# Row sums of a 16384 x 1024 matrix: two load queues, and VectorE adding each row as two halves

## The chip, the cores and the metric

The kernel runs on one core of a Trainium2 chip. The metric is device time in microseconds (us) of one execution; lower is better. Times of several executions are given by their median.

## The reference

```
x: 32 x 512 x 1024 float32, divisor: 1024.0
out = sum(x over the last axis) / divisor        # 32 x 512 float32
```

There are 32 x 512 = 16384 rows of 1024 numbers, 67.1 MB to be read, and 16384 numbers to be written.

## The kernel before

The rows are spread over the 128 partitions, 128 rows to each. "A row" below means one row in every partition: 128 x 1024 float32, 0.524 MB. The 128 rows are split into three parts by their place in DRAM: `x_main` (97 rows, results in `res`), `x_first` (15 rows, results in `res0`) and `x_last` (16 rows, results in `fin`). Within a part, a partition's rows of one load are one contiguous run in DRAM.

The loads are listed in `loads`, in the order of work. The main part is loaded in pieces of 2, 13, five times 14, and 12 rows, the first part in one piece of 15, and the last part in pieces of 9, 4 and 2 rows. Pieces of the main and the first part, and the 9 rows, go round three buffers, `bulk[0]` to `bulk[2]`; the 4 and the 2 rows have buffers of their own, `t4` and `t2`. The very last row comes as two halves, `pa` and `pb`.

All loads are issued by SyncE (SP), on its one queue. The first three are moved by `start_loads_at_once` ahead of everything else in the program (L119 in the profile). Each later load into a `bulk` buffer (L146) waits until VectorE, and ScalarE where it had rows of it, have finished the load that was in that buffer three loads ago. The loads of `t4`, `t2`, `pa` and `pb` (L146 to L148) wait for nothing, but are issued after the 9 rows.

VectorE handles the loads in their order, after a wait for each to land. A piece of the main or the first part is summed by one reduction over all its rows:

```
nc.vector.reduce_sum(out=dst[:, :m], in_=t[:, :m, :], axis=AX).then_inc(dve)      # L191
```

The rows of the last part are summed one by one by `both_halves` (L182): one instruction reads the two halves of a row as two inputs, adds them element by element, scales, writes the sums over the first half, and accumulates them to one number.

ScalarE takes the last few rows of some loads (the second number in the pairs of `main`, `first` and `last`: 3 of the 12, 6 of the 15, 4, 2 and 1 of the last part): an activation with a copy and an accumulated sum into `junk` (L174), one row each.

The sums of the main and the first part are not yet scaled. GpSimd multiplies `res` by 1/divisor (L159) when its rows are done, and `res0` (L163) after that; SyncE waits for each and then issues its store (L150, L152). The last store, of `fin` (L207), waits for VectorE and ScalarE.

Of the kernel before, what the change touches and what calls it, by code (L numbers as in the profile page):

```python
# [7 lines left out]
F32 = mybir.dt.float32  # L8
ADD = mybir.AluOpType.add
COPY = mybir.ActivationFunctionType.Copy  # L10
AX = mybir.AxisListType.X
SP = mybir.EngineType.SP


# [20 lines left out]
@with_exitstack  # L35
def kernel(
    ctx: ExitStack,
    tc: tile.TileContext,
    x: bass.AP,
    divisor: float,  # L40
    out: bass.AP,
):
    nc = tc.nc
    nc.at_finalize(start_loads_at_once)
    xf = x.flatten_outer_dims()
    N, D = xf.shape
    P = nc.NUM_PARTITIONS
    scale = 1.0 / float(divisor)
    J = N // P
    assert J * P == N  # L50

    F, L = 15, 16
    M = J - F - L
    W = M + L
    x_first = bass.AP(tensor=x.tensor, offset=0, ap=[[F * D, P], [D, F], [1, D]])
    x_main = bass.AP(tensor=x.tensor, offset=P * F * D, ap=[[W * D, P], [D, M], [1, D]])
    x_last = bass.AP(tensor=x.tensor, offset=P * F * D + M * D, ap=[[W * D, P], [D, L], [1, D]])
    o_first = bass.AP(tensor=out.tensor, offset=0, ap=[[F, P], [1, F]])
    o_main = bass.AP(tensor=out.tensor, offset=P * F, ap=[[W, P], [1, M]])
    o_last = bass.AP(tensor=out.tensor, offset=P * F + M, ap=[[W, P], [1, L]])  # L60

    def room(name, *shape):
        return nc.alloc_sbuf_tensor(name, [P, *shape], F32).ap()


    base = -(-nc.sbuf_base // 32) * 32
    room("pad", -base % 1024 // 4)
    assert nc.sbuf_base % 1024 == 0
    c = 512
    bulk = [room(f"bulk{i}", r, D) for i, r in enumerate((14, 14, 15))]  # L70
    t4 = room("t4", 4, D)
    t2 = room("t2", 2, D)
    pa = room("pa", c)
    pb = room("pb", D - c + 16)[:, : D - c + 2]
    res0 = room("res0", F)
    res = room("res", M)
    fin = room("fin", L)
    junk = [nc.alloc_psum_tensor(f"junk{i}", [P, D], F32).ap() for i in range(4)]

    loads = []
    sems = {}

    def sem(name):
        sems[name] = nc.alloc_semaphore(name)
        return sems[name]

    in_bulk = [sem(f"in_bulk{i}") for i in range(3)]
    in_t4, in_t2, in_pa, in_pb = (sem(f"in_{n}") for n in ("t4", "t2", "pa", "pb"))  # L90
    out_first, out_main = sem("out_first"), sem("out_main")
    dve, act, pool = sem("by_dve"), sem("by_act"), sem("by_pool")
    landed = nc.alloc_semaphore("landed")

    n = 0
    main = [(2, 0), (13, 0)] + [(14, 0)] * 5 + [(12, 3)]
    first = [(15, 6)]
    last = [(9, 4), (4, 2), (2, 1)]
    assert sum(r for r, _ in first) == F
    assert sum(r for r, _ in main) == M and sum(r for r, _ in last) == L - 1  # L100
    for part, src, dst, by in (
        (main, x_main, res, 1.0), (first, x_first, res0, 1.0), (last, x_last, fin, scale)
    ):
        j = 0
        for rows, on_act in part:
            if rows > 4:
                t, s, slot = bulk[n % 3][:, :rows, :], in_bulk[n % 3], n
                n += 1
            elif part is main:
                t, s, slot = bulk[n % 3][:, :rows, :], in_bulk[n % 3], n  # L110
                n += 1
            else:
                t, s, slot = (t4, in_t4, None) if rows == 4 else (t2, in_t2, None)
            loads.append((t, s, src[:, j : j + rows, :], on_act, dst[:, j : j + rows], by, slot))
            j += rows


    for t, s, src, *_ in loads[:3]:
        i = nc.sync.dma_start(out=t, in_=src).then_inc(s, 16)  # L119
        tc.no_tile_sem_insts.add(i.ins.name)  # L120
    tc.close()
    tc.compile()  # L122


    done_dve, done_act = {}, {}
    d = a = 0
    for k, (t, s, src, on_act, dst, by, slot) in enumerate(loads):
        rows = t.shape[1]
        d += 1 if by == 1.0 else rows - on_act
        a += on_act  # L130
        done_dve[k], done_act[k] = d, a
    arrived, seen = [], {}
    for t, s, *_ in loads:
        seen[s.num] = seen.get(s.num, 0) + 16
        arrived.append(seen[s.num])


    for k, (t, s, src, on_act, dst, by, slot) in enumerate(loads):
        if k < 3:
            continue  # L140
        if slot is not None:
            nc.sync.wait_ge(dve, done_dve[k - 3])
            if done_act[k - 3]:
                nc.sync.wait_ge(act, done_act[k - 3])
            nc.sync.wait_ge(s, arrived[k] - 16)
        nc.sync.dma_start(out=t, in_=src).then_inc(s, 16)  # L146
    nc.sync.dma_start(out=pa, in_=x_last[:, L - 1, :c]).then_inc(in_pa, 16)  # L147
    nc.sync.dma_start(out=pb[:, : D - c], in_=x_last[:, L - 1, c:]).then_inc(in_pb, 16)  # L148
    nc.sync.wait_ge(pool, 2)
    nc.sync.dma_start(out=o_main, in_=res).then_inc(out_main, 16)  # L150
    nc.sync.wait_ge(pool, 3)
    nc.sync.dma_start(out=o_first, in_=res0).then_inc(out_first, 16)  # L152


    nc.gpsimd.memset(pb[:, D - c :], 0.0).then_inc(pool)  # L155
    k = len(main) - 1
    nc.gpsimd.wait_ge(dve, done_dve[k])
    nc.gpsimd.wait_ge(act, done_act[k])
    nc.gpsimd.tensor_scalar_mul(out=res, in0=res, scalar1=scale).then_inc(pool)  # L159
    k += len(first)  # L160
    nc.gpsimd.wait_ge(act, done_act[k])
    nc.gpsimd.wait_ge(dve, done_dve[k])
    nc.gpsimd.tensor_scalar_mul(out=res0, in0=res0, scalar1=scale).then_inc(pool)  # L163


    a = 0
    for k, (t, s, src, on_act, dst, by, slot) in enumerate(loads):
        rows = t.shape[1]
        for r in range(rows - on_act, rows):
            if r == rows - on_act:  # L170
                nc.scalar.wait_ge(s, arrived[k])
            if a >= len(junk):
                nc.scalar.wait_ge(act, a - len(junk) + 1)
            nc.scalar.activation(  # L174
                junk[a % len(junk)], t[:, r, :], COPY, scale=by, accum_out=dst[:, r : r + 1]
            ).then_inc(act)
            a += 1


    def both_halves(dst, src, by):  # L180
        h = src.shape[-1] // 2
        return nc.vector.tensor_tensor_reduce(  # L182
            out=src[:, :h], in0=src[:, :h], in1=src[:, h:], scale=by, scalar=0.0,
            op0=ADD, op1=ADD, accum_out=dst,
        )

    for k, (t, s, src, on_act, dst, by, slot) in enumerate(loads):
        m = t.shape[1] - on_act
        nc.vector.wait_ge(s, arrived[k])
        if by == 1.0:  # L190
            nc.vector.reduce_sum(out=dst[:, :m], in_=t[:, :m, :], axis=AX).then_inc(dve)  # L191
        else:
            for r in range(m):
                both_halves(dst[:, r : r + 1], t[:, r, :], by).then_inc(dve)
    nc.vector.wait_ge(in_pa, 16)
    nc.vector.wait_ge(pool, 1)
    both_halves(pb[:, D - c : D - c + 1], pa, 1.0).then_inc(dve)
    d += 1
    nc.vector.wait_ge(in_pb, 16)
    nc.vector.wait_ge(dve, d)  # L200
    both_halves(fin[:, L - 1 :], pb, scale).then_inc(dve)
    d += 1


    nc.sync.wait_ge(dve, d)
    nc.sync.wait_ge(act, a)
    nc.sync.dma_start(out=o_last, in_=fin).then_inc(landed, 16)  # L207
    for s in (out_first, out_main):
        nc.sync.wait_ge(s, 16)
    ids = [s.num for s in sems.values()]  # L210
    assert max(ids) - min(ids) + 1 == len(ids)
    nc.sync.sem_clear(range(min(ids), max(ids) + 1))
    nc.sync.wait_ge(landed, 16).then_inc(landed, -16)
# [35 lines left out]
```

## Time and profile before

| what | us |
|---|---|
| three runs, median (lowest to highest) | 160.63 (160.36 to 160.64) |
| the profiled execution | 160.41 |
| its span, from first to last instruction | 159.1 |
| VectorE (DVE) busy, 29 instructions | 117.1 |
| ScalarE (ACT) busy, 33 instructions | 18.5 |
| GpSimd (POOL) busy, 7 instructions | 1.0 |
| one reduction of 14 rows on VectorE | 15.1 |
| one row on ScalarE, activation alone | 1.01 |

The profile page counts the time in which an engine works as busy; waits, branches and the issuing of DMAs are not counted. Lines of groups name the source line, the engine, the operation, what is written and read, with partitions x elements, and in square brackets the idle time just before and what ended it. "SPq" is SyncE's own instruction queue, which issues the DMAs. The chain of waits follows the work back from the last instruction, at each step to what released it.

### The profile page before, as it was taken

To read this page: it belongs to the slowest core of one execution; us is meant where nothing else is said; L and a number is where in the kernel's file an instruction comes from. 1 tells how busy PE (TensorE), PEld (TensorE's weight loads), DVE (VectorE), ACT (ScalarE), POOL (GpSimd) and SP (SyncE) were. 2 spreads that over 40 slices of the span, in tenths; PEclk is the share of its full clock that TensorE was granted. 3 is DMA by queue.
4 is the path that set the end of the run, shared out by engine and by line. 5 is a ranking of instruction groups with operands and counts; after the bars stand their busy time and mean duration, and the time that the engine had idled before them with its cause. 6 is when DMAs were issued, how large, how long until landed. Compare 5 with 4: busy or idle time off the path is not lost.

```text
span 159.1 us, 141 instructions
## 1 busy us (share of the span) xinstructions
DVE 117.1 (74%) x29; ACT 18.5 (12%) x33; POOL 1.0 (1%) x7
## 2 busy tenths in 40 slices
DVE  0500089966999599959996899959999960399743
ACT  3000000000000000000000000000008000392684
POOL 0000000000000000000000000000000010000000
DMA  7999969999999699999997899999995999699894
GB/s 286 459 482 455 453 303 461 461 461 461 461 461 433 288 433 461 461 461 461 461 447 332 375 461 461 461 396 395 482 556 247 494 494 494 297 445 445 371 410 159
DMA packets 2448, 67.18 MB, mean 422 GB/s; under 512 B 656, under 2 KB 656, under 8 KB 912
## 3 DMA queue, kind: packets, MB, share of 16 engines
q1 hardware_dynamic: 2448, 67.18, 98.2%
HBM read 67.11 MB, written 0.07 MB: 422 GB/s over the span
## 4 chain that ended last, share of the span: by engine, by line
DMA 77%; DVE 21%; SPq 1%; issue 0%
DMA bulk<-in_x_dram 55%; DMA pb<-in_x_dram 22%; DVE res L191 20%; SPq L146 1%; SPq L147 0%; DVE pb L182 0%; DVE fin L182 0%
## 5 line engine op out<-in xcount | busy, mean ns | idle before, releaser
L191 DVE TENSOR_REDUCE res<-bulk 128x14 f32<-128x14336 f32 (+3 forms) x9 | 111.2, 12360 | 36.3 <-DMA bulk<-in_x_dram 36.3
L174 ACT ACTIVATE junk<-bulk 128x1024 f32<-128x1024 f32 x13 | 13.1, 1010 | 135.3 <-DMA bulk<-in_x_dram 135.3
L182 DVE CUSTOM_DVE_ANT_0 t<-t 128x512 f32<-128x512 f32 x3 | 2.0, 689 | 2.9 <-DMA t<-in_x_dram 2.9
L182 DVE CUSTOM_DVE_ANT_0 bulk<-bulk 128x512 f32<-128x512 f32 x5 | 3.1, 689 | 1.1 <-DMA bulk<-in_x_dram 1.1
L174 ACT ACTIVATE junk<-t 128x1024 f32<-128x1024 f32 x3 | 3.1, 1021 | 0.9 <-DMA t<-in_x_dram 0.9
L174 ACT ACTIVATION_READ_ACCUMULATOR junk<-bulk 128x1 f32 x13 | 2.4, 186 | 0.0
L174 ACT ACT_TABLE_LOAD x1 | 1.3, 1283 | 2.4 <-PEq L122 2.4
L159 POOL TENSOR_SCALAR res<-res 128x97 f32<-128x97 f32 x1 | 0.5, 465 | 127.4 <-DVE res L191 127.4
L182 DVE DVE_READ_ACCUMULATOR2_ANT fin<- 128x1 f32 x9 | 0.7, 82 | 0.0
L174 ACT ACTIVATION_READ_ACCUMULATOR junk<-t 128x1 f32 x3 | 0.6, 187 | 0.0
L182 DVE CUSTOM_DVE_ANT_0 pb<-pb 128x257 f32<-128x257 f32 x1 | 0.4, 427 | 0.2 <-DMA pb<-in_x_dram 0.2
L182 DVE CUSTOM_DVE_ANT_0 pa<-pa 128x256 f32<-128x256 f32 x1 | 0.4, 425 | 0.0
L163 POOL TENSOR_SCALAR res<-res 128x15 f32<-128x15 f32 x1 | 0.3, 262 | 17.3 <-DVE res L191 17.3
L155 POOL MEMSET pb<- 128x2 f32 x1 | 0.1, 99 | 2.0 <-POOLq L122 2.0
L230 POOL MEMSET const-bfloat16-1.0<- 128x1 bf16 x1 | 0.1, 101 | 0.0
L230 POOL MEMSET const-uint8-127<- 128x1 uint8 x1 | 0.1, 101 | 0.0
L230 POOL MEMSET const-float32-0.0<- 128x1 f32 x1 | 0.1, 99 | 0.2 <-issue 0.2
L230 POOL MEMSET const-float32-1.0<- 128x1 f32 x1 | 0.1, 98 | 0.0
L182 DVE DVE_READ_ACCUMULATOR2_ANT pb<- 128x1 f32 x1 | 0.1, 80 | 0.0
## 6 DMA issues: line engine op xcount, KB each, us to landing
bulk<-in_x_dram SPq DMA_DIRECT2D x5, 7168.0 KB, 36.4
bulk<-in_x_dram SPq DMA_DIRECT2D x1, 7680.0 KB, 34.5
bulk<-in_x_dram SPq DMA_DIRECT2D x1, 6656.0 KB, 19.9
bulk<-in_x_dram SPq DMA_DIRECT2D x1, 6144.0 KB, 33.2
bulk<-in_x_dram SPq DMA_DIRECT2D x1, 4608.0 KB, 28.4
t<-in_x_dram SPq DMA_DIRECT2D x1, 2048.0 KB, 32.9
bulk<-in_x_dram SPq DMA_DIRECT2D x1, 1024.0 KB, 4.7
t<-in_x_dram SPq DMA_DIRECT2D x1, 1024.0 KB, 34.9
```

Of the source, the lines that this page charges most:

```text
L146: nc.sync.dma_start(out=t, in_=src).then_inc(s, 16)
L155: nc.gpsimd.memset(pb[:, D - c :], 0.0).then_inc(pool)
L159: nc.gpsimd.tensor_scalar_mul(out=res, in0=res, scalar1=scale).then_inc(pool)
L163: nc.gpsimd.tensor_scalar_mul(out=res0, in0=res0, scalar1=scale).then_inc(pool)
L174: nc.scalar.activation(junk[a % len(junk)], t[:, r, :], COPY, scale=by, accum_out=dst[:, r : r + 1]).then_inc(act)
L182: return nc.vector.tensor_tensor_reduce(out=src[:, :h], in0=src[:, :h], in1=src[:, h:], scale=by, scalar=0.0, op0=ADD, op1=ADD, accum_out=dst,
L191: nc.vector.reduce_sum(out=dst[:, :m], in_=t[:, :m, :], axis=AX).then_inc(dve)
L230: nc = _bacc.Bacc("TRN2", target_bir_lowering=False, num_devices=1)
```

## The change

Loads are now issued by two engines. The list `order` names for each load its queue, SyncE (`sp`) or ScalarE (`sc`), its part, its rows and how many of them are ScalarE's. The first load is 7 rows from SyncE; then 14-row loads alternate between ScalarE and SyncE; the 15 rows of `x_first` are the last load of ScalarE's queue, and 6 rows of the main part follow on SyncE's. The loads of the last part are as before, on SyncE's queue. The three buffers go round as before, so a load waits for VectorE to finish the load three places ahead of it in `order`, on the engine that issues it. Of the first three loads the two on SyncE are moved ahead of the program; ScalarE's first one is not.

VectorE sums every row with `both_halves`, already scaled. ScalarE keeps only the rows of the last part. GpSimd's two multiplications go, and the stores of `res` and `res0` wait for VectorE instead.

```diff
-    bulk = [room(f"bulk{i}", r, D) for i, r in enumerate((14, 14, 15))]
+    bulk = [room(f"bulk{i}", r, D) for i, r in enumerate((14, 15, 14))]
...
-    main = [(2, 0), (13, 0)] + [(14, 0)] * 5 + [(12, 3)]
-    first = [(15, 6)]
-    last = [(9, 4), (4, 2), (2, 1)]
...
+    sp, sc = nc.sync, nc.scalar
+    order = [(sp, x_main, res, 7, 0)]
+    order += [(sc, x_main, res, 14, 0), (sp, x_main, res, 14, 0)] * 3
+    order += [(sc, x_first, res0, 15, 0), (sp, x_main, res, 6, 0)]
+    order += [(sp, x_last, fin, 9, 4), (sp, x_last, fin, 4, 2), (sp, x_last, fin, 2, 1)]
...
-    for t, s, src, *_ in loads[:3]:
+    early = [k for k, load in enumerate(loads[:3]) if load[0] is sp]
+    for k in early:
+        _, t, s, src, *_ = loads[k]
         i = nc.sync.dma_start(out=t, in_=src).then_inc(s, 16)
...
-        if slot is not None:
-            nc.sync.wait_ge(dve, done_dve[k - 3])
-            if done_act[k - 3]:
-                nc.sync.wait_ge(act, done_act[k - 3])
-            nc.sync.wait_ge(s, arrived[k] - 16)
-        nc.sync.dma_start(out=t, in_=src).then_inc(s, 16)
+        if slot is not None and k > 2:
+            queue.wait_ge(dve, done_dve[k - 3])
+            queue.wait_ge(s, arrived[k] - 16)
+        queue.dma_start(out=t, in_=src).then_inc(s, 16)
     nc.sync.dma_start(out=pa, in_=x_last[:, L - 1, :c]).then_inc(in_pa, 16)
     nc.sync.dma_start(out=pb[:, : D - c], in_=x_last[:, L - 1, c:]).then_inc(in_pb, 16)
-    nc.sync.wait_ge(pool, 2)
+    nc.sync.wait_ge(dve, max(done_dve[k] for k, load in enumerate(order) if load[2] is res))
     nc.sync.dma_start(out=o_main, in_=res).then_inc(out_main, 16)
-    nc.sync.wait_ge(pool, 3)
     nc.sync.dma_start(out=o_first, in_=res0).then_inc(out_first, 16)
...
-    nc.gpsimd.tensor_scalar_mul(out=res, in0=res, scalar1=scale).then_inc(pool)
...
-    nc.gpsimd.tensor_scalar_mul(out=res0, in0=res0, scalar1=scale).then_inc(pool)
...
         nc.vector.wait_ge(s, arrived[k])
-        if by == 1.0:
-            nc.vector.reduce_sum(out=dst[:, :m], in_=t[:, :m, :], axis=AX).then_inc(dve)
-        else:
-            for r in range(m):
-                both_halves(dst[:, r : r + 1], t[:, r, :], by).then_inc(dve)
+        for r in range(t.shape[1] - on_act):
+            both_halves(dst[:, r : r + 1], t[:, r, :], scale).then_inc(dve)
```

## The prediction

> **What bounds the kernel now.** I read the chain of waits first, then the order of time on VectorE, then the DMA parts of the page, each to answer one question: what ends last, is the thing that ends last ever idle, and what would have to be late for the end to move.
>
> The chain, its last pieces (start, length, what):
>
> ```profile
> 105.00 15.10 DVE res L191
> ...
> 121.97 35.17 DMA pb<-in_x_dram
> 157.15 0.02 issue
> 157.17 0.43 DVE pb L182
> 157.60 0.01 DVE fin L182
> ```
>
> The last half row lands at 157.15 and VectorE needs 0.43 us more. The 20% of VectorE in this chain is not a price: the chain passes through a reduction because a load was issued when it ended, but that load then lay in the queue for 35 us. Whether it delayed any data is seen in the landings. In the timeline, VectorE's start after a wait on a DMA is a landing:
>
> ```profile
> 4.72 2.29 DVE L191 TENSOR_REDUCE res<-bulk 128x2 f32<-128x2048 f32 x1 [4.72 <-DMA bulk<-in_x_dram]
> ...
> 37.30 15.09 DVE L191 TENSOR_REDUCE res<-bulk 128x14 f32<-128x14336 f32 x1 [2.89 <-DMA bulk<-in_x_dram]
> ...
> 105.00 24.75 DVE L191 TENSOR_REDUCE res<-bulk 128x14 f32<-128x14336 f32 x2 [1.83 <-DMA bulk<-in_x_dram]
> ...
> 148.58 0.69 DVE L182 CUSTOM_DVE_ANT_0 bulk<-bulk 128x512 f32<-128x512 f32 x1 [1.10 <-DMA bulk<-in_x_dram]
> 149.20 0.08 DVE L182 DVE_READ_ACCUMULATOR2_ANT fin<- 128x1 f32 x1
> 149.20 0.69 DVE L182 CUSTOM_DVE_ANT_0 bulk<-bulk 128x512 f32<-128x512 f32 x1
> ```
>
> From 37.30 to 105.00 four loads of 14 rows land: 67.70 / 56 = 1.209 us a row (a row here is one row in each of 128 partitions, 0.524 MB, so 434 GB/s). All 128 rows at that pace take 154.7 us. The first load of 2 rows landed at 4.72 where 2.42 us of streaming would do, so starting cost 2.30 us. 2.30 + 154.7 = 157.0, and the last data came at 157.15. Nothing was lost between: loads stream without a gap that can be measured, and VectorE waits for every load (1.8 us before each of the 14-row ones). The page says the same in its own way:
>
> ```profile
> DVE 117.1 (74%) x29; ACT 18.5 (12%) x33; POOL 1.0 (1%) x7
> ...
> DMA packets 2448, 67.18 MB, mean 422 GB/s; under 512 B 656, under 2 KB 656, under 8 KB 912
> ...
> q1 hardware_dynamic: 2448, 67.18, 98.2%
> ```
>
> The transfers fill 98.2% of the span. (The dips to 6 and 7 in the slices of DMA do not stand in the landings, so I do not count them as idle.) Of 2448 packets 912 are under 8 KB; the other 1536 are 12 loads times 128 partitions, so a packet is a partition's whole piece of a load: 56 KB for 14 rows. That matters below.
>
> So the kernel is bound by streaming, and the time can only move in three ways: the pace of 1.209 changes, the stream runs dry, or something is late behind the last data. What is fixed now: 2.3 start, 154.7 stream, 0.45 VectorE, 1.4 for the store (issued at 157.63) to land. The span is 159.08, the profiled execution 160.41, so 1.33 lies outside the span. The median of the three runs is 160.63, 0.14% above that; I work on the profiled time and give the forecast on the median.
>
> **The change, part by part.**
>
> *VectorE, two halves at once.* The five rows from 148.58 follow each other at 0.61 us ((151.03 - 148.58) / 4), and the last ends 0.70 after its start. A 14-row load takes 13 x 0.61 + 0.70 = 8.7 us instead of 15.1; 15 rows 9.3; 7 rows 4.4; 6 rows 3.8. In all 120 rows, about 74 us instead of 117. Worth on the path: 0, since the stream is the cover: VectorE already waits before each load. It frees a buffer 6.4 us earlier, which starts nothing earlier, as the queue was never empty. Without this cover the tail below would be priced.
>
> *GpSimd's scaling.* Two multiplies of 0.47 and 0.26 us at 129.83 and 147.63 and their hand-over go. They only released the two stores of results, which lay behind the last input loads on the queue (landing 27.2 and 9.8 us after issue). Worth 0.
>
> *ScalarE's rows.* The 9 single rows of the 12- and 15-row loads go to VectorE. Worth 0, as above; the 7 rows of the last part stay.
>
> *Start.* SyncE still issues at 0.0, now 7 rows and 14 rows. ScalarE's first load cannot be issued before 2.38 (its first instruction now), or 3.66 if behind the table load of 1.28 us. The 7 rows alone stream until 2.3 + 8.5 = 10.8, so ScalarE's first load is there in time even with 2.3 us of start. Worth 0.
>
> *Two queues at once.* This is the unknown: no row of the trace shows two queues with loads in both. If they take turns packet by packet, each time one packet of either, I step through it by rows (ScalarE's first load in effect from 5.9, 3.0 rows of load 0 being through; landing times): load 0 has 4.6 of 8 packets left, each round is 7/8 + 14/8 rows, 12.1 rows, 20.5. Load 1 has 3.4 packets left against load 2: 11.9 rows, 34.9. Then with 14 rows on both sides the steps alternate: 4.6 rounds of 3.5 rows = 19.5 us, 3.4 rounds = 14.4 us. Load 2 54.4, 3 68.8, 4 88.2, 5 102.6, load 6 (against 15 rows) 122.8. Load 7, the 15 rows on ScalarE's queue, has 3.4 packets left against load 8's 6 rows: 8.9 rows, 133.6. Load 8 alone then lands at 137.8, which is 112 rows x 1.209 + 2.3, so no row is lost. Does a queue run dry? Load k+3 is issued 8.7 us after load k lands; load 3 is there at 24.9 and wanted at 34.9, loads 5 and 7 are there 5.7 us before they are wanted, load 9 at 122.8 + 8.7 = 131.5, 6.3 us before load 8 lands, against 2.3 of start. So it never does. Loads 9 to 11 and the last two halves then have the order, the queue and the place they have now: 148.6, 153.4, 155.9, 157.15. VectorE ends load 7 at 142.9 and load 8 at 146.7, before 148.6. The two stores on SyncE, now behind VectorE's load 8, are issued near 147 (now 130.33 and 147.92), still behind the last inputs on the same queue; the last store waits behind them on SyncE and needs them issued by 157.6, ten us later. On ScalarE the last load is issued near 97 and its first row of the tail comes at 148.6, so the wait queued ahead of it holds up nothing. Worth 0 in all: 160.41 + 0.
>
> *What a turn costs.* The nearest rows are boundaries between loads on one queue. The 2-row load took 155.93 - 153.43 = 2.50 us, 0.08 over 2 x 1.209; the 4 rows took 4.85, 0.01 over. So a load's 8 packets cost some 0.01 to 0.1 us beyond their bytes. Nine loads now share the stream, 0.9 us at most. Two queues could hide that (down 0.9) or pay it once more at each turn (up 0.9). A far upper end is a whole start, 2.3 us, for each of the eight later ones, 18 us; the landings on one queue show starts hidden behind other data, which leaves it no weight. I take 0, nearest to the 4-row load.
>
> [...]
>
> **The rivals.**
>
> *Equal bytes (slower).* If the two queues share the pace evenly whatever their packets, ScalarE's load 7 comes too late for the order in which VectorE takes them. Same steps with half pace for each: load 0 15.6, 1 39.8, 2 49.5, 3 73.7, 4 83.4, 5 107.6, 6 117.3. By then 4 rows of load 7 are through; load 8's 6 rows finish at 131.8, and load 7's last 5 rows, sharing with load 9, take 12.1 more: 143.9. All data still arrives by 157.15, but VectorE has 15 + 6 + 5 + 2 + 1 = 29 rows behind that landing, 17.8 us, and 0.8 for the two halves: 162.5 instead of 157.6. That is +4.9, 165.3. With ScalarE's start earlier or shorter, load 7 comes near 142.4: +3.4, 163.8. It decides from the point where load 7 lands after 157.6 - 18.6 = 139.0; by packets it is 5.4 us below that. For it speaks that the 7-row first load makes a half-load offset only under equal shares; against it that a packet here is 24 to 60 KB and a unit of its own in the count.
>
> *The boundaries hide in each other (faster).* Down to 159.5 if all 0.9 is won; more is not there, as start, bytes and the last store stay. For it: short loads do cost more than their bytes. Against: the pace of the 14-row loads, 1.209, holds steady, with no gap to fill.
>
> *Each turn costs (slower).* Up to 161.3 by the same 0.9; it would show in the pace alone, with VectorE on time.
>
> **How the numbers follow.** A measurement of this kernel can tell about 0.2%, 0.32 us, from no change. Unchanged end: 0.39. Hidden boundaries: 0.16. Paid turns: 0.15. Equal bytes: 0.26. The remaining 0.04 is for a queue that does run dry in a way I have not seen, slower. So faster 0.16, same 0.39, slower 0.45. The likeliest single case gives 160.41 on the profiled execution, 160.6 on the median; its own range is 160.3 to 160.9. The forecast range goes from 159.9, leaving the lower half of the faster case out, to 165.2, which takes in paid turns and nearly all of equal bytes.
>
> **What would show it.** Right: VectorE's busy time near 75 us; loads 9, 10 and 11 starting near 148.6, 153.4 and 155.9 with VectorE waiting for each; the chain ending in the DMA of pb near 157.15; the DMA share still at 98%. Equal bytes: VectorE starting load 7 after 139 and then working through to the end without a wait, the chain ending in VectorE's rows and not in DMA, and a landing near 132 for the 6 rows before the 15. A paid turn: pb landing after 157.5 with a pace above 1.209. I am wrong altogether if the landings are spaced so that the stream stands idle between two of them.

## The result and the profile after

The changed kernel takes 162.0 us (median of four runs, 161.95 to 162.32) against 160.5 us beside it: a ratio of 1.0097, 95% interval 1.008 to 1.0115. It is slower by 1.5 us. The forecast's likeliest case, no change at 160.6, did not hold. The forecast gave slower 0.45, nearly all of it for equal bytes (0.26) and paid turns (0.15). The time lies inside the range, but the mechanism that lengthened it is none of the rivals, so that the range held is luck. The profiled execution took 162.32, the longest of the four; its span is 161.0, 1.9 us longer than the span before.

The page of the changed kernel, the parts that answer to those shown of before (busy time by engine; then the queues with packets, MB and share):

```profile
span 161.0 us, 331 instructions
...
DVE 75.3 (47%) x244; ACT 8.9 (6%) x15; POOL 0.3 (0%) x5
...
q1 hardware_dynamic: 1872, 37.29, 54.4%
q10 hardware_dynamic: 576, 29.88, 42.9%
q14 instruction: 2, 0.02, 0.0%
```

VectorE is down to 75.3 us as forecast, but its instructions went from 29 to 244. And there is a third queue that the page of before does not have: q14, kind "instruction", 2 packets, 0.02 MB. It is two fetches of program code in the middle of the run. By share it is nothing, and that is what makes it easy to read past.

The end of the chain of waits of the changed kernel (start, length, what):

```profile
134.97 24.08 DMA pb<-in_x_dram
159.05 0.02 issue
159.08 0.43 DVE pb L165
159.50 0.01 DVE fin L165
```

Nothing has changed in kind: the last half row lands, VectorE adds 0.43 us, the store goes. It lands at 159.05 instead of 157.15, and those 1.90 us are the loss between the two profiled executions (1.5 by the medians). So the streaming ends late although the bytes are the same. The landings on VectorE (timeline, first instruction after a wait) show where in time it happened:

```profile
34.59 0.69 DVE L165 CUSTOM_DVE_ANT_0 bulk<-bulk 128x512 f32<-128x512 f32 x1 [8.34 <-DMA bulk<-in_x_dram]
...
134.91 0.69 DVE L165 CUSTOM_DVE_ANT_0 bulk<-bulk 128x512 f32<-128x512 f32 x1 [1.79 <-DMA bulk<-in_x_dram]
...
150.32 0.69 DVE L165 CUSTOM_DVE_ANT_0 bulk<-bulk 128x512 f32<-128x512 f32 x1 [2.46 <-DMA bulk<-in_x_dram]
```

Load 1 comes at 34.6, as stepped through in the prediction (34.9). Load 7 comes at 134.9 instead of 133.6, load 9 at 150.3 instead of 148.6. But these landings are those of the slowest of 16 DMA engines: the trace has 16 reports for a load, and of load 7's 15 came by 133.62 and the last at 134.89. What the 16 do at the very end is read from the busy shares in stretches. First the changed kernel, then the kernel before (stretch, its length, busy time of VectorE, ScalarE and GpSimd, clock, DMA share, GB/s):

```profile
156.50:157.10 0.60, 0.00 (x0) 0.60 (x1) 0.00 (x0) 1.00 0.81 233
157.10:157.70 0.60, 0.00 (x0) 0.26 (x2) 0.00 (x0) 1.00 0.16 48
157.70:158.30 0.60, 0.50 (x1) 0.50 (x1) 0.00 (x0) 1.00 0.06 24
158.30:159.10 0.80, 0.59 (x5) 0.65 (x2) 0.00 (x0) 1.00 0.06 17
```

```profile
156.50:157.10 0.60, 0.51 (x4) 0.58 (x2) 0.00 (x0) 1.00 0.69 168
157.10:157.70 0.60, 0.43 (x2) 0.00 (x0) 0.00 (x0) 1.00 0.00 0
```

Before, all transfers are over by 157.1. In the changed kernel nearly all are over by then too, and from 157.7 to 159.1 the share is 0.06: one engine of 16 (1/16 = 0.0625). Fifteen engines ended nearly on time; one was behind, and pb did not land before that one was through (15 of its 16 reports came by 157.68, the last at 159.05).

That one engine carried the two fetches. The packet records of the trace name no DMA engine, but on the loads each record starts within some nanoseconds of the end of another, so they can be joined from end to start into 16 chains, one for each engine. (Where two records end together, two chains can be swapped; when the chains end does not change by that.) The end of a chain's last large packet (over 20 KB) shows how far that engine is behind:

| kernel | packets of 8 KB on q14 | 15 chains (14 in the last line) | the others |
|---|---|---|---|
| before | 0 | 147.86 to 148.20 | 148.26 |
| changed | 2 | 147.90 to 148.79 | 149.86 |
| changed, one queue | 2 | 147.90 to 148.42 | 149.59 |
| changed, one fetch left | 1 | 147.96 to 148.44 | 148.98 |
| before, 512 memsets | 4 | 147.94 to 148.18 | 150.47 |
| before, 1024 memsets | 8 | 147.81 to 148.14 | 152.84 |
| changed, 512 memsets | 2 and 4 | 147.89 to 148.43 | 149.94 and 150.64 |

(The lines below the second are runs of the next section.) Wherever there are fetches, the chain that ends last holds all of them; in the last line each of two chains holds the fetches of one issuing engine.

When they came fits the instructions. The trace has them at 46.35 and 129.48, each 8 KB and 0.31 us long. At the first, VectorE had done 21 rows (loads 0 and 1), at the second 85 (loads 0 to 5 and 8 rows of load 6). Between them lie 64 rows of two instructions, 128 instructions (an estimate of 64 bytes each, by 8 KB). In the trace's packet records the data packet that follows each fetch takes 0.53 and 0.56 us longer than its size otherwise does (2.647 instead of 2.116 us for 56 KB, 1.476 instead of 0.912 for 24 KB), so a fetch puts that engine back by 0.31 + 0.55, some 0.85 us; twice that is 1.7 of the 1.9 us.

### The profile page after: what moved, and what is told of

The parts are those of the page before. It is cut to its first block, busy times and chain, and to the rows that moved or that the text cites. A ratio compares the mean times of both kernels' runs of the same rounds, so it can differ in the third digit from the quotient of the medians.

```text
span 161.0 us, 331 instructions
## 1 busy us (share of the span) xinstructions
DVE 75.3 (47%) x244; ACT 8.9 (6%) x15; POOL 0.3 (0%) x5
## 4 chain that ended last, share of the span: by engine, by line
DMA 84%; DVE 14%; SPq 1%; issue 0%
DMA bulk<-in_x_dram 69%; DMA pb<-in_x_dram 15%; DVE bulk L165 13%; SPq L138 1%; SPq L139 0%; DVE pb L165 0%; DVE res L165 0%; DVE fin L165 0%
## 5 line engine op out<-in xcount | busy, mean ns | idle before, releaser
L165 DVE CUSTOM_DVE_ANT_0 bulk<-bulk 128x512 f32<-128x512 f32 x117 | 72.4, 686 | 81.0 <-DMA bulk<-in_x_dram 81.0
L165 DVE DVE_READ_ACCUMULATOR2_ANT res<- 128x1 f32 x112 | 9.1, 81 | 0.0
L157 ACT ACTIVATE junk<-bulk 128x1024 f32<-128x1024 f32 x4 | 4.0, 1012 | 50.0 <-DMA bulk<-in_x_dram 50.0
L157 ACT ACTIVATION_READ_ACCUMULATOR junk<-bulk 128x1 f32 x4 | 0.7, 187 | 0.0
```

Source lines behind the costliest of these rows:

```text
L157: nc.scalar.activation(junk[a % len(junk)], t[:, r, :], COPY, scale=scale, accum_out=dst[:, r : r + 1]).then_inc(act)
L165: return nc.vector.tensor_tensor_reduce(out=src[:, :h], in0=src[:, :h], in1=src[:, h:], scale=by, scalar=0.0, op0=ADD, op1=ADD, accum_out=dst,
```

## The experiments

Theory F (fetch): the loss is VectorE's longer program, fetched over one of the DMA engines that the loads need. Theory T (turns): it is the alternation of the two queues, which lets the engines drift apart. Theory A (access): VectorE's two reads and one write for each pair of numbers slow the transfers.

**Queues back to one**, VectorE's part of the change kept (on the changed kernel):

```diff
-    sp, sc = nc.sync, nc.scalar
+    sp, sc = nc.sync, nc.sync
```

> The changed kernel with all its loads on SyncE's queue; VectorE's row-by-row sums stay. Theory F (instruction fetch): VectorE's 244 instructions are fetched during the run in two 8 KB packets through the same transfers, each puts one of the 16 DMA engines some 0.85 us back, and a load has landed only when the last engine is through. Then the queues are innocent: 162.0 us as changed, two packets on q14, pb landing near 159. Theory T (turns): alternating between two queues lets the engines drift apart; then one queue gives 160.5 us and pb at 157.2. Theory A (access): VectorE's two reads and one write per element slow the transfers; also 162.0, but by pace of all loads.

Measured: 161.86 us, ratio 1.0084 (1.007 to 1.0097). pb lands at 158.53. Its page:

```profile
DVE 75.2 (47%) x244; ACT 8.9 (6%) x15; POOL 0.3 (0%) x5
...
q1 hardware_dynamic: 2448, 67.18, 97.4%
q14 instruction: 3, 0.02, 0.0%
```

Of the three packets on q14 one is of 24 bytes at the start; two are of 8 KB, at 37.62 and 119.23. With one queue nearly all of the loss stays (1.36 of 1.5 us), so T falls as its cause.

**VectorE's program back to its size**, two queues kept (on the changed kernel):

```diff
+    n_red, acts = 9, {6: 6, 7: 6}
...
+        m = t.shape[1] - on_act
+        if k < n_red:
+            nc.vector.reduce_sum(out=dst[:, :m], in_=t[:, :m, :], axis=AX).then_inc(dve)
+            continue
...
+    nc.gpsimd.tensor_scalar_mul(out=res, in0=res, scalar1=scale).then_inc(pool)
+    nc.gpsimd.tensor_scalar_mul(out=res0, in0=res0, scalar1=scale).then_inc(pool)
...
```

`acts` names the rows of loads 6 and 7 that ScalarE takes. They are left unscaled too, and SyncE's stores wait for GpSimd.

> The changed kernel with its two queues and its loads, but loads 0 to 8 summed by one reduction each as before (6 rows of load 6 and 6 of load 7 go to ScalarE so that the stream never runs dry, GpSimd scales the two results): VectorE has as few instructions as before. F: 160.5 us, no packet on q14 in the span, pb near 157.2. T: 162.0 us, pb near 159. A: 160.5 us.

Measured: 160.78 us, ratio 1.0017 (1.0008 to 1.0026). Its page and the end of its chain:

```profile
DVE 113.7 (71%) x29; ACT 21.6 (14%) x39; POOL 1.6 (1%) x7
...
q1 hardware_dynamic: 1872, 37.29, 54.9%
q10 hardware_dynamic: 576, 29.88, 43.3%
```

```profile
157.37 0.02 issue
157.40 0.43 DVE pb L174
```

No q14, pb at 157.37, 1.2 of the 1.5 us gone. A small excess of 0.28 us stays. This run does not tell F from A, which both forecast it.

**The fourth corner, and the second once more.** The same reductions with the one-line edit of the first experiment:

> The run with two queues and one reduction per load, with all its loads on SyncE's queue: the fourth corner beside the changed kernel, its one-queue version and the two-queue reductions. Two queues with reductions cost 0.28 us over the kernel before. If the turns cost that: 160.5 us here. If it comes from the sizes of the loads, the rows moved to ScalarE or the later scaling: 160.8 us here as well.

> The two-queue reductions once more beside it, on the same chip: 160.8 us if the small excess of 0.17% over the kernel before is real, 160.5 us if it was that chip's.

Measured on one chip, beside 160.48 for the kernel before: one queue 160.67, ratio 1.0006 (0.9997 to 1.0016); two queues 160.78, ratio 1.002 (1.0011 to 1.0029). The small excess came again, and 160.67 lies between the two forecasts for one queue: what it comes from is not settled. So, with the changed kernel's list of loads:

| median us | one queue | two queues |
|---|---|---|
| a reduction per load, 29 VectorE instructions | 160.67 | 160.78 |
| row by row, 244 VectorE instructions | 161.86 | 162.0 |

The lower row was measured beside 160.50. Down a column 1.2 us, along a row 0.1 us. The two queues as such cost 0.1 us, which single comparisons cannot tell from none. A column differs in more than instructions (reductions, rows of ScalarE, scaling), and A would forecast it too. The landings tell A from F. With one queue and the same loads, row by row first, then with reductions:

```profile
27.83 0.69 DVE L165 CUSTOM_DVE_ANT_0 bulk<-bulk 128x512 f32<-128x512 f32 x1 [12.54 <-DMA bulk<-in_x_dram]
45.28 0.69 DVE L165 CUSTOM_DVE_ANT_0 bulk<-bulk 128x512 f32<-128x512 f32 x1 [8.79 <-DMA bulk<-in_x_dram]
...
131.94 0.69 DVE L165 CUSTOM_DVE_ANT_0 bulk<-bulk 128x512 f32<-128x512 f32 x1 [10.43 <-DMA bulk<-in_x_dram]
```

```profile
27.95 15.09 DVE L183 TENSOR_REDUCE res<-bulk 128x14 f32<-128x14336 f32 x1 [9.26 <-DMA bulk<-in_x_dram]
44.86 15.09 DVE L183 TENSOR_REDUCE res<-bulk 128x14 f32<-128x14336 f32 x1 [1.83 <-DMA bulk<-in_x_dram]
...
130.79 16.21 DVE L183 TENSOR_REDUCE res<-bulk 128x9 f32<-128x9216 f32 x2 [9.54 <-DMA bulk<-in_x_dram]
```

Up to the first fetch (37.62) the row-by-row kernel's loads are not late (27.83 against 27.95). Behind it they are 0.4 us late and stay 0.3 us late up to 112.85 (against 112.56); behind the second (119.23) they are 1.15 us late. That is a step at each fetch and no slower pace, and 15 of the 16 chains end on time: A falls.

**Fewer fetches.** On the changed kernel, loads 0 to 3 by one reduction each, GpSimd scaling those 49 columns; `n_red` is 4 in place of 9, and no rows are moved to ScalarE:

> The changed kernel with loads 0 to 3 (49 rows) summed by one reduction each, scaled by GpSimd; the other 71 rows stay row by row. F: 148 VectorE instructions, the second fetch of the changed kernel came 64 rows after the first, so one packet on q14 is left: half of the loss, 161.2 us. T: 162.0 us. A: in proportion to the rows, 160.5 + 1.5 x 71/120 = 161.4 us, which this run alone does not tell from F, but without a step in the landings.

Measured: 161.11 us, ratio 1.0036 (1.0023 to 1.0049); one packet on q14, pb at 157.89. One fetch less takes 0.9 us off, the remaining one, at 110.04, costs 0.33 us over the two-queue reductions.

**Instructions alone, on an engine that does nothing.** This is the kernel before with idle GpSimd running memsets into a buffer that nobody reads. Neither queues, loads nor VectorE's work are touched, so here T and A have nothing to say:

```diff
+    dust = room("dust", 512)
...
+    for i in range(512):
+        nc.gpsimd.memset(dust[:, i : i + 1], 0.0)
```

> The kernel before, with 512 memsets of one column on GpSimd, which is idle, into a buffer nobody reads: 512 more instructions and no other work. F: 32 KB of instructions at 8 KB a fetch, some of it held already: 3 to 4 packets on q14. If all use one DMA engine, 3 x 0.85 to 4 x 0.85 us: 163.0 to 163.9. If each used another engine, 161.3. T and A: 160.5 us.

Measured: 162.83 us, ratio 1.0144 (1.0131 to 1.0158). From its page:

```profile
DVE 117.1 (73%) x29; ACT 18.5 (11%) x33; POOL 18.7 (12%) x519
...
q1 hardware_dynamic: 2448, 67.18, 96.9%
q14 instruction: 4, 0.03, 0.0%
```

The memsets are over by 26 us and the kernel ends 2.3 us later: 0.58 us a fetch, all four on one engine (the chains above). Twice as many, `range(1024)`:

> The kernel before with 1024 one-column memsets on GpSimd, twice those of the run with 512, which had 4 packets on q14 and cost 2.3 us. F: one packet for each 128 instructions, so 8 packets, all on one DMA engine, 8 x 0.58 = 4.7 us: 165.2 us. If a later fetch goes to another engine or hides, less; if GpSimd's work itself disturbed the loads, time would follow its busy time, also doubled, which the run with few wide memsets tells apart.

Measured: 165.52 us against 160.39 beside it, ratio 1.032 (1.0302 to 1.0338), 8 packets on q14 (page) and a stretch at the end in which one engine works alone for 2.7 us and more:

```profile
q14 instruction: 8, 0.07, 0.1%
```

```profile
158.30:161.00 2.70, 1.41 (x5) 2.28 (x5) 0.00 (x0) 1.00 0.06 26
```

That is 5.1 us for eight fetches, 0.64 each. GpSimd's own timeline falls into blocks of 128 memsets, such as these:

```profile
15.96 4.44 POOL L158 MEMSET dust<- 128x1 f32 x128 [2.10 <-issue]
27.38 4.44 POOL L158 MEMSET dust<- 128x1 f32 x128 [0.42 <-issue]
```

The profile names no cause for the idle time before them. But a fetch's packet starts 1.65 us before each of the two (at 14.31 and 25.74), so it reads as GpSimd waiting for its code.

The control, more elements but few instructions, 80 memsets of 20 columns:

> The kernel before with 80 memsets of 20 columns on GpSimd: three times the elements written by the run with 512, but under 128 instructions. F: no packet on q14, 160.5 us. If writing by GpSimd beside the loads were the cost: over 162.8 us by elements, or 160.9 us by instructions (80/512 of 2.3 us).

Measured: 160.60 against 160.39 us, ratio 1.001 (0.9998 to 1.0022). Here F was wrong in one point: there is one packet on q14. So here a fetch did not wait for 128 instructions to be used up; GpSimd, with 87 counted by the page, already drew the next 8 KB, at 7.97 us. Its cost cannot be told from none. With three times the elements of the 512 memsets and a small part of their cost, the cost does not follow what GpSimd writes. GpSimd is also busy for less time here, 4.6 us instead of 18.7, and by busy time some 0.5 us would be lost, not far from what this run can tell; the chains settle it, since with the memsets only the one DMA engine with the fetches is late.

**Two engines with long programs.** The changed kernel with the 512 memsets on GpSimd:

> The changed kernel with the 512 one-column memsets on GpSimd. VectorE's two fetches cost 1.5 us, GpSimd's four 2.3 us. If both engines' fetches go over the same DMA engine, they add: 164.3 us. If each has a DMA engine of its own, the later of the two ends it: 162.8 to 163.1 us.

Measured: 162.9 us against 160.39, ratio 1.0154 (1.0139 to 1.0169). Six packets on q14, and at the end:

```profile
157.70:158.30 0.60, 0.00 (x1) 0.34 (x3) 0.00 (x0) 1.00 0.11 41
158.30:159.10 0.80, 0.80 (x3) 0.80 (x1) 0.00 (x0) 1.00 0.11 38
```

A share of 0.11 instead of 0.06: two DMA engines are late, side by side. VectorE's and GpSimd's fetches went over different DMA engines here (chains ending at 149.94 and 150.64); the two delays did not add (162.9 us, against 162.83 with the memsets alone), the larger one counted.

**A try at a faster kernel.** With the fetches out, both kernels are at the end of the stream, so only what follows the last landing is left. The kernel before with the last row split at three quarters:

```diff
-    c = 512
+    c = 768
```

> The kernel before with its last row in pieces of three quarters and one quarter instead of two halves: what VectorE adds after the last data has landed falls from 257 to 129 elements, 0.43 to some 0.30 us. 160.4 us, 0.1% below the kernel before, at the edge of what can be told; pb still lands at 157.15.

Measured: 160.64 us, ratio 1.0016 (1.0008 to 1.0025): slower by 0.25 us. The end of its chain shows why the end came later although the last instruction got shorter (0.29 us):

```profile
156.84 0.56 DVE pa L182
...
157.45 0.02 DVEq L200
157.47 0.08 issue
157.55 0.29 DVE pb L182
```

The last quarter waits at L200 for VectorE's sum of the three quarters (0.56 us instead of 0.43 for a half), not for its own landing. Of the kernels run here, none beats the kernel before.

## Why the prediction was wrong

**The step that failed** is "VectorE, two halves at once ... Worth on the path: 0". It weighed the change of VectorE by time only (74 instead of 117 us) and named the stream as the cover. The measured cost of that step is 1.2 us, by both columns of the table. It has 244 instructions instead of 29, which stood in the terms of the sum (120 rows, two lines of the timeline per row) and was never asked what it does. The assumption behind it, that VectorE's program reaches the chip without the loads' help, was not stated.

**What the prediction had right.** What bounds the kernel: the stream's end sets the time in every run above but the last, which waits for a sum behind it. The turns by packet: load 1 at 34.6 (34.9 forecast) and load 7 at 134.9 (133.6), where equal bytes would have put them at 39.8 and 143.9. So the rival of equal bytes fell, and with it the price of 3.4 to 4.9 us. That the two queues take turns by whole packets was an assumption of the author's, which no run had shown before the result; the packet records of the changed kernel show it: from ScalarE's first packet to its last, 54 of 61 neighbours on each of the 16 chains are of different queues. The landings do not all fit the steps so closely: SyncE's loads 0, 2, 4 and 6 came at 21.9, 56.1, 89.9 and 124.5, 1.4 to 1.7 us after the steps, the first of them before any fetch. One reading behind the steps was wrong: ScalarE's first load was issued at 1.92, not at 2.38 or later. Whether the lateness comes from that is not shown; it cost nothing, since every chain of packets of the changed kernel runs from 3 to 156 us without a gap. VectorE's busy time came to 75.3 us (about 74 forecast), the stores were issued at 147.9 (near 147 forecast), and the stream never ran dry. GpSimd's scaling and ScalarE's rows, both priced at 0, were not run alone.

**A term whose size is settled.** The cost of a turn, bounded at 0.9 us up and down and taken as 0, came out at 0.1 us on two pairs (160.78 - 160.67 and 162.0 - 161.86). Neither hidden boundaries nor paid turns, the two rivals that turned on it, is seen. pb did land after 157.5, one half of the sign for paid turns; the other half, a pace above 1.209, did not come: from load 3 to load 5 it is (102.60 - 68.81) / 28 = 1.207.

**What the view could have shown.** Both facts were in reach before: that the transfers have no slack (98.2%), and that VectorE's instructions grow eightfold. What was not in the trace was a q14 in the span, so the price itself could not have been read.

**Why a single fetch is cheap.** By its own engine's packets, GpSimd's first fetch costs 0.31 + 0.21 us and each later one 0.31 + 0.35: eight come to 5.1 us, as measured, and four to 2.5 (measured 2.3). VectorE's two cost 0.84 and 0.87. But a delayed engine counts only as far as it ends behind the others, and these end some 0.4 us apart without any fetch (147.86 to 148.26). So the one fetch of 0.84 us left its engine only 0.54 us behind the next one (148.98 against 148.44), and 0.33 us in the medians. Beside the 80 memsets the engine with the fetch ended at 148.32, the next at 148.15, and nearly all of the 0.52 is hidden.

**What stays open.** Why the data packet behind a fetch takes longer, and why by 0.53 to 0.56 us behind VectorE's fetches and by 0.21 to 0.35 behind GpSimd's. The runs give the price, not the reason. The excess of 0.2 to 0.3 us of the reductions over the kernel before is open too.

## What to carry to other kernels

In a kernel whose transfers never rest, count instructions as well as time: here a long unrolled program was itself loaded by DMA during the run, at some 0.6 us for every 128 instructions (0.58 and 0.64 us a fetch with 512 and 1024 memsets), on one DMA engine that all loads waited for. Look for a queue of kind "instruction" in the page, and at the DMA share in the last stretches: here a share of 0.06, 1/16, was one engine that fell behind. In such a kernel an engine's slack in time is not by itself a reason to trade few long instructions for many short ones.

## What the runs showed of the hardware that was not expected

- Program code shared the DMA engines with the data, and in these runs one issuing engine's fetches all fell on one of them: with 1024 memsets one engine was alone at work to the end (share 0.06), and one chain of packets holds all eight fetches. In the run with both, fetches of VectorE and of GpSimd fell on two (0.11).
- In the changed kernel 128 VectorE instructions lie between the two fetches (64 rows of two, between 46.35 and 129.48); GpSimd drew four with 512 memsets and eight with 1024, 8 KB each. One was drawn with 87 instructions, so it reads as asked for ahead of need. It also reads as not always there in time: with 1024 memsets, two of GpSimd's blocks of 128 start after 2.10 and 0.42 us of idle time. In this kernel, bound by its loads, the fetches were not hidden: 0.58 and 0.64 us each with 512 and 1024 memsets.
- A DMA engine that was put back did not catch up while the loads never rested: with 512 memsets the delay of fetches up to 26 us still stands at the end, where that engine's chain ends 2.3 us behind the next (150.47 against 148.18).
